# Where K and Q projections stand among the short convolutions of an encoder layer, and two small edits at the start and in the feed-forward part

## The chip, the core and the metric

The kernel runs on one core of a Trainium2 chip. Its engines work side by side, each on its own instruction stream: TensorE (matmuls, and transposes as matmuls), VectorE, ScalarE and GpSimd (element work), SyncE (which here issues the DMA transfers). The metric is the device time of one execution in microseconds (us). In the listings PE is TensorE, PEld its weight loads, DVE VectorE, ACT ScalarE, POOL GpSimd, and SPq SyncE's queue of transfers. L330 is line 330 of the kernel; lines of the changed kernel lie two or three higher, since the change adds lines.

## The reference

One encoder layer on 1024 tokens with 16 learned tokens set before them, width 1024, everything in 32-bit floats:

```python
h_res = concat([meta, x])                       # 1040 x 1024
h = rmsnorm(h_res, norm1_w)
proj = h @ w_in                                 # q k v z | beta, a | sc_b sc_c sc_x | gate_a gate_b
# branch A, per head (8 heads of 128), forward and backward:
qkv = silu(conv5(concat[q, k, v])); q, k = l2norm(q) * 128**-0.5, l2norm(k)
beta = sigmoid(b_raw); g = -exp(A_log) * softplus(a_raw + dt_bias)
o = scan(forward) + flip(scan(backward))        # chunks of tokens, state S 128 x 128:
    #   v_new = u - w @ S;  o_c = q_dec @ S + qk @ v_new;  S = S * gl + k_dec.T @ v_new
o_dn = rmsnorm(o) * dn_norm_w * silu(z)
# branch B and the merge
y_b = sc_b * conv3(sc_c * sc_x)
merged = sigmoid(gate_a) * (o_dn @ w_branch_dn) + sigmoid(gate_b) * (y_b @ w_branch_sc)
h_res += merged @ w_out
gu = rmsnorm(h_res, norm2_w) @ w_gate_up        # 2 x 2816 columns
h_res += (silu(gu[:, :2816]) * gu[:, 2816:]) @ w_down
out = rmsnorm(h_res, final_norm_w)[16:]
```

## The kernel before

**Precision.** A 32-bit product is done as three matmuls of a reduced type: each operand is split in a high part (a cast, on ScalarE) and a low part (the original less the high part, on VectorE; helper `split`, L86 and L87), and high x high, high x low and low x high are summed. So each piece of weights or activations passes both element engines once before TensorE can use it.

**Stages.** (1) The start: nine tiles of tokens are loaded, their root mean square taken (`root`, ScalarE and GpSimd), scaled in place (`scaled`, VectorE, L1019), transposed on TensorE (`turned`, L83) and split (`highs`, `lows`, L1038 and L1044). (2) The first part: all columns of the input projection, the convolutions, the scans of branch A. (3) One late gate (`dense`, L119 to L121) and the products of the branches and of the merge, in seven block products (`seven`, L1379). (4) The output projection and second norm (L1593 to L1595). (5) The feed-forward part, first half: 22 units of 128 pairs of hidden columns, each with seven products (`product`, L1653 to L1655). (6) Second half: the product with `w_down` (L1808 to L1810), also in seven block products, and the last norm.

**The first part** is emitted in an order that a planner in the kernel works out when the program is built: the manual schedule keeps it, and each engine runs its instructions in that order. The planner has a clock per engine (`T`), advanced by estimated costs. The projection is cut into *units* of 128 columns: for each of 8 heads a K, a Q and a V unit (`u_qkv`, numbers i = 0, 1, 2), and *fill units*: z per head, then for each of 8 column blocks three units of the short convolution (`u_short`, i = 0, 1, 2: the factor under the convolution, its partner, and the factor outside), then the gates (`u_gate`). `pick` (L921) chooses the next unit. In the kernel before it takes the next K, Q or V unit when `qkv_ok` allows it, and never between the three units of one short convolution (`mid`). `qkv_ok` lets a head begin only below `near + 3`, where `near` counts the scans that have reached round `NEAR`.

While a unit's matmuls are emitted (`dense_steps`, L330, eight steps per chunk of tokens), the planner sets pieces of other work between the steps: `run_streams` emits the streams of branch A (decay, norms, the triangular inverse, and the scan `g_scan` in 8 rounds per head), and `pump` (L296) emits VectorE work from four lanes: `conv` (the five-tap convolution of a K, Q or V unit, L353), `short` (the three-tap one), `fs` and `norm`. Among the lanes that are ready `pump` takes the one on which the least time has been spent so far. A third short-conv unit reads the finished convolution when its product is read out, and emits what is left of it at once if need be (`force`). The weights of a unit are fetched two units ahead, and split in four parts during the unit before (`split_part`, casts L941 on ScalarE and differences L938 on VectorE).

A round of the scan does, on TensorE, S times K and S times Q (L794, L797); on VectorE the rest `r` for both directions (L804); on TensorE the product with the inverse (L812); on ScalarE two scalings (L819 and the one after); on TensorE the two products L829 and L832; on VectorE the new state (L841) and the sums of the output. After the last round the output is scaled by its norm (L891, ScalarE), after a fixed delay of the planner's clock (L886), transposed (L83), multiplied with the gate z (L897) and stored (L900).

**Down sums.** In the feed-forward part, units 2 to 12 also prepare differences of rows of `w_down` for the last stage: `down_sums` (L1671) loads two rows of 128 x 1024 into a tile `sums`, does four differences on VectorE (L141) and stores them. Behind the first part the framework's scheduler sets each engine's order, by when it reckons an instruction's inputs ready: it may put work of a later unit ahead, and a new tile may be loaded as soon as its memory is free, so the first `down_sums`, which stand in the code of unit 2, are found among the instructions of unit 0. In units 0, 1 and 2 VectorE also makes the sums and differences of the unit's own weights (`sums`, L141 on `raw`; line L1631 for the first) and their splits.

## Time and profile before

| what | us |
|---|---|
| time, median of 3 runs | 1969.58 (1968.12 to 1970.8) |
| profiled execution | 1968.53 |
| its span, first to last instruction | 1966.8 |
| TensorE busy | 1943.5 (99%) |
| VectorE busy | 1468.4 (75%) |
| ScalarE busy | 868.7 (44%) |
| GpSimd busy | 159.2 (8%) |

The mean granted clock of TensorE is 0.999. The page gives the busy time of each engine; a table by windows gives it for stretches of the span; the waits are given by the instruction that waited, what released it, the total, how often and the longest; a timeline has, for each instruction or run of like instructions, the start, the duration, the engine, the line, what is written and read, and in brackets how long the engine stood idle before it and who released it. Matmuls are pipelined: a matmul of 512 columns is listed with some 0.39 us while the next one starts 0.23 us after it. So time lost between two matmuls is read from their starts: the distance, less what it is at full rate.

### The profile page before, as it was taken

How to read it: one execution, taken by the hardware profiler on the slowest of the kernel's cores; microseconds unless marked ns; L12 is line 12 of the kernel's file. 1: busy time of each engine (PE TensorE's matmuls, PEld its weight loads, DVE VectorE, ACT ScalarE, POOL GpSimd, SP SyncE). 2: the span in 40 equal slices, each digit the busy share in tenths (PEclk: the TensorE clock that was granted, in tenths of full speed). 3: DMA queues.
4: the chain of work that ended last, by engine and by line, in shares of the span. 5: the costliest groups of instructions: out<-in, count | busy, mean ns of one | idle time of the engine just before them, and what ended most of it. 6: DMA issues, size and time to landing. Idle time of an engine off the chain costs nothing.

```text
span 1966.8 us, 31940 instructions
## 1 busy us (share of the span) xinstructions
PE 1943.5 (99%) x11962; PEld 1703.1 (87%) x11962; DVE 1468.4 (75%) x2801; ACT 868.7 (44%) x2013; POOL 159.2 (8%) x457
## 2 busy tenths in 40 slices
PE   8999999999999999999999999999999999999998
PEld 8998899999999999998878888887888888888887
DVE  4778787879788878777458798559876887856574
ACT  5563554555555464533345545234332332324343
POOL 3012112011020202010000000000000000000001
PEclk9999999999999999999999999999999999999999
DMA  4222332323122223225287523333655545587654
GB/s 145 67 76 81 103 97 60 87 60 86 50 90 65 79 56 87 66 70 173 76 295 268 202 95 118 110 126 123 231 195 194 187 157 171 173 280 240 195 178 159
DMA packets 243136, 264.11 MB, mean 134 GB/s; under 512 B 46820, under 2 KB 166933, under 8 KB 240549
## 3 DMA queue, kind: packets, MB, share of 16 engines
q1 hardware_dynamic: 242981, 262.07, 41.8%
q8 instruction: 94, 1.54, 0.3%
q14 instruction: 61, 0.50, 0.1%
HBM read 189.58 MB, written 72.44 MB: 133 GB/s over the span
## 4 chain that ended last, share of the span: by engine, by line
PE 93%; DVE 3%; ACT 2%; issue 1%; DMA 0%; POOL 0%; SPq 0%; POOLq 0%; DVEq 0%; ACTq 0%
PE pm L330 34%; PE pm L1379 5%; PE pd L1379 4%; PE pe L1379 3%; PE pm L1653 2%; PE pm L1655 2%; PE pm L1654 2%; PE pd L1653 2%; PE pd L1655 2%; PE pd L1654 2%; PE pe L1655 2%; PE pe L1653 2%; PE pe L1654 2%; PE pd L812 2%; PE pe L581 2%; PE pm L1809 1%
## 5 line engine op out<-in xcount | busy, mean ns | idle before, releaser
L330 PE MATMUL pm<-hTh,wh 128*128 128x320 f32 (+4 forms) x1328 | 485.2, 366 | 0.1
L330 PE MATMUL pm<-hTh,wl 128*128 128x320 f32 (+4 forms) x1328 | 451.0, 340 | 0.0
L330 PE MATMUL pm<-al,wh 128*128 128x320 f32 (+4 forms) x1328 | 450.3, 340 | 0.5 <-DVE al L1044 0.5
L330 PEld LDWEIGHTS pm<-hTh,wl 128*128 128x128 f32 x1328 | 249.4, 188 | 15.4
L330 PEld LDWEIGHTS pm<-hTh,wh 128*128 128x128 f32 x1328 | 250.7, 189 | 13.5 <-ACT hTh L1038 0.2
L330 PEld LDWEIGHTS pm<-al,wh 128*128 128x128 f32 x1328 | 250.8, 189 | 13.1 <-DVE al L1044 0.7
L87 DVE TENSOR_TENSOR al<-raw,ring_h 128x1024 fp32r<-128x1024 f32 x73 | 88.4, 1223 | 64.3 <-ACT ring_h L86 54.6
L86 ACT CAST ring_h<-raw 128x1024 fp32r<-128x1024 f32 x73 | 76.8, 1053 | 110.4 <-PE pd L1810 35.7
L938 DVE TENSOR_TENSOR wl<-raw,wh 128x512 fp32r<-128x512 f32 x122 | 84.0, 690 | 45.7 <-ACT wh L941 45.1
L353 DVE SCALAR_TENSOR_TENSOR kq<-ra,wc,kq 128x520 f32<-128x520 f32 (+1 forms) x128 | 96.4, 753 | 3.0 <-ACT kq L387 1.2
L819 ACT ACTIVATE w<-pd,small 128x128 f32<-128x128 f32 x128 | 40.0, 364 | 97.1 <-PE pd L812 81.3
L128 POOL TENSOR_SCALAR ss<-ss 128x1 f32<-128x1 f32 x13 | 4.6, 351 | 934.8 <-ACT b L1820 605.0
L489 DVE TENSOR_TENSOR tm<-fP,fN 128x135 f32<-128x135 f32 (+23 forms) x248 | 72.2, 291 | 8.8 <-POOL mP L661 2.5
L493 DVE TENSOR_TENSOR fP<-fP,tm 128x135 f32<-128x135 f32 (+23 forms) x248 | 71.7, 289 | 7.4
L941 ACT CAST wh<-raw 128x512 fp32r<-128x512 f32 x122 | 74.5, 618 | 0.9 <-PE pm L330 0.8
L86 ACT CAST raw<-pair 128x1024 fp32r<-128x1024 f32 (+1 forms) x42 | 41.7, 993 | 56.5 <-PE pd L1379 26.0
L87 DVE TENSOR_TENSOR wl<-pair,wh 128x1024 fp32r<-128x1024 f32 (+1 forms) x42 | 48.2, 1148 | 22.3 <-ACT wh L86 22.2
L841 DVE SCALAR_TENSOR_TENSOR S<-S,eGl,pd 128x128 f32<-128x128 f32 x104 | 31.9, 345 | 43.9 <-PE pd L829 29.6
L87 DVE TENSOR_TENSOR raw<-pair,raw 128x1024 fp32r<-128x1024 f32 (+1 forms) x42 | 48.2, 1147 | 19.4 <-ACT raw L86 19.3
L130 POOL TENSOR_TENSOR small<-small,minus_half 128x9 f32<-128x9 f32 x16 | 29.9, 1870 | 404.8 <-DVE small L876 251.6
L86 ACT CAST wh<-pair 128x1024 fp32r<-128x1024 f32 (+1 forms) x42 | 41.7, 992 | 43.6 <-PE pd L1379 23.2
L1334 DVE TENSOR_TENSOR b<-pm,b 128x512 f32<-128x512 f32 x58 | 39.1, 686 | 21.2 <-PE pm L1655 19.0
(659 smaller groups left out, 4950.0 us busy)
## 6 DMA issues: line engine op xcount, KB each, us to landing
raw<-in_w_in_dram SPq DMA_DIRECT2D x64, 512.0 KB
raw<-in_w_gate_up_dram SPq DMA_DIRECT2D x44, 512.0 KB
sums<-in_w_down_dram SPq DMA_DIRECT2D x22, 512.0 KB
t_d<-sums SPq DMA_DIRECT2D x11, 1024.0 KB
raw<-s_d SPq DMA_DIRECT2D x44, 256.0 KB
raw<-t_d SPq DMA_DIRECT2D x44, 256.0 KB
act_d<-b SPq DMA_DIRECT2D x43, 256.0 KB
raw<-act_d SPq DMA_DIRECT2D x33, 256.0 KB
```

The lines of the kernel that those rows point to most:

```text
L86: nc.scalar.copy(hi, src)
L87: nc.vector.tensor_tensor(out=lo, in0=src, in1=hi.bitcast(F32), op=ALU.subtract)
L330: mm(po[:, :n], (wl if j == 2 else wh)[:, k], xl[k][:, t0:t0 + n] if j == 1 else xh[k][:, t0:t0 + n], start=(i == 0), stop=(i == 3 * KT - 1))
L353: nc.vector.scalar_tensor_tensor(out=acc, in0=raw[:, h0 + t:h0 + t + hn], scalar=wc[:, t, col:col + 1], in1=acc, op0=ALU.mult, op1=ALU.add)
L489: nc.vector.tensor_tensor(out=tv, in0=fP[:, 0:r, j:j + 1].broadcast_to([P, r, n]), in1=fN[:, j:j + 1, j + 1:32].broadcast_to([P, r, n]), o ...
L493: nc.vector.tensor_tensor(out=fP[:, 0:r, j + 1:32], in0=fP[:, 0:r, j + 1:32], in1=tv, op=ALU.subtract)
L938: nc.vector.tensor_tensor(out=u[1][1][:, k], in0=u[2][:, k], in1=u[1][0][:, k].bitcast(F32), op=ALU.subtract)
L941: nc.scalar.copy(u[1][0][:, k], u[2][:, k])
L1379: mm(bank[t], a[:, c], b, start=fresh, stop=first and k == 3 and j == 2, skip_group_check=not first)
L1653: mm(po, ah[:, k], bhk, start=k == 0, stop=False)
L1654: mm(po, ah[:, k], blk, start=False, stop=False)
L1655: mm(po, al[:, k], bhk, start=False, stop=k == 3)
```

## The change

It has four groups of edits.

1. *Order in the first part.* `pump` leaves the lane `short` aside whenever another lane is ready. K and Q units may now stand between the three units of a short convolution, a V unit still not. `near` counts scans that reached round 3 instead of 5, so that a head's units may begin earlier. A K unit takes its two tiles after its first chunk's matmuls instead of before them.
2. *Output of a head.* The delay before the last scaling on the planner's clock is 2300 instead of 1500.
3. *Start.* The first three tiles of tokens are scaled in two halves of 512 columns.
4. *Down sums.* The first `down_sums` (of unit 2) writes two elements of its new tile from `sg`, the result of that unit, before it loads the tile; so this load, and all that follows it in that tile, comes after that result.

```diff
@@ pump
+            if len(cand) > 1 and "short" in cand:
+                cand.remove("short")
             k = min(cand, key=lambda q: spent[q])
@@ u_qkv
-        if i == 0:
-            while freed < h - 2:
-                T["pe"] += 100
-                yield
-            st_["kq"] = d1.tile([P, 2, L], F32, tag="kq", name=uid("kq"), bufs=3)
-            st_["vT"] = d1.tile([P, L], F32, tag="vT", name=uid("vT"), bufs=2)
...
             yield from dense_steps(po, w, hx, t0, n, sweep=(h == i == ci == 0))
             if raw is None:
+                if i == 0:
+                    while freed < h - 2:
+                        T["pe"] += 100
+                        yield
+                    st_["kq"] = d1.tile([P, 2, L], F32, tag="kq", name=uid("kq"), bufs=3)
+                    st_["vT"] = d1.tile([P, L], F32, tag="vT", name=uid("vT"), bufs=2)
+                dst = (st_["kq"][:, 0], st_["kq"][:, 1], st_["vT"])[i]
@@ g_scan
-        yield T["dve"] + 1500
+        yield T["dve"] + 2300
@@ units
-    NEAR = 5
+    NEAR = 3
@@ pick
-        if qkv_units and not mid and qkv_ok():
+        if qkv_units and qkv_ok() and not (mid and qkv_units[0][3] == 2):
@@ scaled
-            nc.vector.scalar_tensor_tensor(out=xs[t][:p], in0=xs[t][:p], scalar=rss[t][:p, 1:2], in1=w1row[:p],
-                                           op0=ALU.mult, op1=ALU.mult)
+            for c in (slice(0, 512), slice(512, 1024)) if t < 3 else (slice(0, D),):
+                nc.vector.scalar_tensor_tensor(out=xs[t][:p, c], in0=xs[t][:p, c], scalar=rss[t][:p, 1:2], in1=w1row[:p, c],
+                                               op0=ALU.mult, op1=ALU.mult)
@@ down_sums
-    def down_sums(k):
+    def down_sums(k, behind=None):
...
+        if behind is not None:
+            nc.scalar.copy(r[:1, :, 0:1], behind[:1, 0:2].unsqueeze(2))
@@ loop over the feed-forward units
-            down_sums(j - 2)
+            down_sums(j - 2, sg if j == 2 else None)
```

With these, the order of units per head goes from S0 S1 S2 K Q V to S0 S1 K Q S2 V in the middle of the first part (S0 to S2 are the three units of a short convolution). Three places are shown as each engine has its instructions in order.

The first is VectorE in the V unit of a head in the middle of the first part, at one round of the scan: L804 makes r, L938 is the low half of the next unit's weights, L489 and L493 are steps of the norm stream, L865 a sum of the output. Before:

```order
L865 TENSOR_TENSOR NP_1845<-pd_4201,NP_1845 128x128
L489 TENSOR_TENSOR tm_4287<-fP_3804,fN_3803 128x136
L938 TENSOR_TENSOR wl_4168<-raw_3925,wh_4167 128x512
L804 SCALAR_TENSOR_TENSOR r_657_4299<-pd_4293,negEG,vS_3437 128x128
L804 SCALAR_TENSOR_TENSOR r_658_4301<-pd_4293,negEG,vS_3437 128x128
L493 TENSOR_TENSOR fP_3804<-fP_3804,tm_4287 128x8x17
```

And in the changed kernel, at the V unit of the same head:

```order
L867 TENSOR_TENSOR NP_1848<-pd_4084,NP_1848 128x128 x2
L491 TENSOR_TENSOR tm_4163<-fP_3865,fN_3864 128x184
L806 SCALAR_TENSOR_TENSOR r_619_4177<-pd_4168,negEG,vS_3463 128x128
L806 SCALAR_TENSOR_TENSOR r_620_4179<-pd_4168,negEG,vS_3463 128x128
L495 TENSOR_TENSOR fP_3865<-fP_3865,tm_4163 128x8x23
L940 TENSOR_TENSOR wl_4106<-raw_3939,wh_4105 128x512
```

The weight difference stood ahead of both r; now it stands behind them.

The second is SyncE at the end of the first part: L455 stores a gate, L900 the last head's output, L810 loads z, L1343 loads the first blocks of the branch products. Before:

```order
L455 DMA tb_d_99<-rb_12191 128x512
L810 DMA vS_11402<-z_d_108 128x1024
L455 DMA tb_d_99<-rb_12250 128x512
L900 DMA o_d_116<-NP_10419 128x4x128 x2
L1343 DMA pair_12285<-in_w_in_dram 128x4x512
```

And in the changed kernel:

```order
L457 DMA tb_d_98<-rb_12175 128x512
L902 DMA o_d_116<-NP_10325 128x4x128 x2
L457 DMA tb_d_98<-rb_12222 128x512
L457 DMA tb_d_99<-rb_12250 128x512
L457 DMA tb_d_99<-rb_12278 128x512
L1346 DMA pair_12288<-in_w_in_dram 128x4x512
```

The output's two stores stood last before the block's load; now three gate stores lie between them. On TensorE 3 projection matmuls followed the last L832 of the last scan; now 99 do, and the last head's eight transposes, which stood among the late gate's matmuls, stand among these.

The third is VectorE at the passage from unit 0 to unit 1 of the feed-forward part: L1334 adds a product's bank to a running sum, L1657 multiplies the sum by its SiLU gate, L1631 and L141 on `raw` are the sums of unit 1's weights, and L87 on `s_hl` is the low half of these. Before:

```order
L1334 TENSOR_TENSOR b_2391_14775<-pd_14932,b_2391_14775 128x512
L1631 TENSOR_TENSOR raw_14815<-raw_14815 128x512
L1657 TENSOR_TENSOR b_2391_14775<-b_2391_14775 128x512
L1334 TENSOR_TENSOR b_2391_14775<-pd_14933,b_2391_14775 128x512 x2
L141 TENSOR_TENSOR raw_14815<-raw_14814,raw_14815 128x512
L87 TENSOR_TENSOR w_2418_14911<-raw_14852,w_2418_14911 128x512
L1334 TENSOR_TENSOR b_2391_14775<-pd_14934,b_2391_14775 128x512
L141 TENSOR_TENSOR raw_14814<-raw_14815,raw_14814 128x512
L87 TENSOR_TENSOR s_hl_15006<-raw_14815,s_hl_15006 128x1024
```

And in the changed kernel:

```order
L1634 TENSOR_TENSOR raw_14818<-raw_14818 128x512
L141 TENSOR_TENSOR raw_14818<-raw_14817,raw_14818 128x512
L1337 TENSOR_TENSOR b_2391_14778<-pd_14935,b_2391_14778 128x512
L141 TENSOR_TENSOR raw_14817<-raw_14818,raw_14817 128x512
L1660 TENSOR_TENSOR b_2391_14778<-b_2391_14778 128x512
L1337 TENSOR_TENSOR b_2391_14778<-pd_14936,b_2391_14778 128x512 x2
L141 TENSOR_TENSOR raw_14817<-raw_14817 128x512
L1337 TENSOR_TENSOR b_2391_14778<-pd_14937,b_2391_14778 128x512
L87 TENSOR_TENSOR s_hl_15009<-raw_14818,s_hl_15009 128x1024
```

The sums of the weights on `raw` stand one or two additions earlier, and two steps of down sums (L141 on `sums`) that stood just ahead of the piece shown are gone from there.

More of the change, by code (lines that the diff above doesn't have):

```diff
@@ L367, in u_qkv @@
         st_ = heads[h]
-        if i == 0:
-            while freed < h - 2:
-                T["pe"] += 100
-                yield
-            st_["kq"] = d1.tile([P, 2, L], F32, tag="kq", name=uid("kq"), bufs=3)
-            st_["vT"] = d1.tile([P, L], F32, tag="vT", name=uid("vT"), bufs=2)
         col = (8 + h, h, 16 + h)[i]
-        dst = (st_["kq"][:, 0], st_["kq"][:, 1], st_["vT"])[i]
         raw = None
```

## The prediction, on record before the changed kernel ran

> **What bounds the kernel now.** I read the first part of the page, then the busy time of each engine by stage, then the waits of TensorE in total, and last the order of time at each wait. The profiled execution took 1968.53 us; its span is 1966.8 us, and 1.7 us lie around it.
>
> ```profile
> span 1966.8 us, 31940 instructions
> PE 1943.5 (99%) x11962; PEld 1703.1 (87%) x11962; DVE 1468.4 (75%) x2801; ACT 868.7 (44%) x2013; POOL 159.2 (8%) x457
> ```
>
> TensorE is the bound. The change adds and removes no matmul, so it can only win back time in which TensorE stood still. Where that time lies, by stage (start, first part with the projections, three branch products, entry of the feed-forward part, rest):
>
> ```profile
> 0.00:16.00 16.00, 11.14 (x81) 10.19 (x81) 6.69 (x10) 9.40 (x16) 5.35 (x15) 1.00 0.91 282
> 16.00:1002.00 986.00, 977.63 (x7613) 902.05 (x7613) 750.35 (x1897) 492.44 (x1536) 138.31 (x410) 1.00 0.29 82
> 1002.00:1340.00 338.00, 337.83 (x1525) 280.53 (x1526) 258.08 (x296) 155.29 (x204) 7.44 (x16) 1.00 0.50 170
> 1340.00:1362.00 22.00, 19.07 (x80) 14.31 (x80) 22.00 (x32) 8.18 (x13) 0.00 (x0) 1.00 0.19 62
> 1362.00:1967.00 605.00, 597.82 (x2667) 495.99 (x2665) 431.29 (x570) 203.43 (x249) 8.13 (x17) 1.00 0.60 199
> ```
>
> The columns are TensorE, its weight loads, VectorE, ScalarE and GpSimd busy, then the clock. TensorE's idle time is 4.9, 8.4, 0.2, 2.9 and 7.2 us; the clock is full everywhere. The last 7.2 us are the end of the program, which no edit touches. What is left to win is about 16 us, under 1%. In the fourth row VectorE is busy for all 22 us: there it is the bound. The waits by whom TensorE waited for (total, times, longest):
>
> ```profile
> PE pd L812 <- DVE r L804: 2.9, 5, 1.0
> PE pd L83 <- DVE xr L1019: 2.6, 3, 1.4
> PE pe L1653 <- ACT mA L86: 1.0, 1, 1.0
> ```
>
> **The change, part by part.** *First part: pump's rule, the place of K and Q units, NEAR.* These move instructions; none is added. A round of the scan needs VectorE's r before its product L812:
>
> ```profile
> 350.38 0.31 PE L330 MATMUL pm<-al,wh 128*128 128x320 f32 x1
> 350.53 0.31 PE L330 MATMUL pm<-hTh,wl 128*128 128x320 f32 x1
> 350.55 0.69 DVE L938 TENSOR_TENSOR wl<-raw,wh 128x512 fp32r<-128x512 f32 x1 [1.60 <-ACT wh L941]
> 351.16 0.60 DVE L804 SCALAR_TENSOR_TENSOR r<-pd,negEG,vS 128x128 f32<-128x128 f32 x2
> 351.81 0.60 PE L812 MATMUL pd<-r,NP 128*128 128x128 f32 x3 [0.98 <-DVE r L804]
> 452.88 0.60 PE L812 MATMUL pd<-r,NP 128*128 128x128 f32 x3 [0.98 <-DVE r L804]
> ```
>
> VectorE stood idle for 1.60 us behind a weight split L938 whose ScalarE half came late (ScalarE first emptied a chunk of V), and r stood behind it. The lost time is more than 0.98: starts at full rate are 350.53 - 350.38 = 0.15 us apart, here 1.28, so 1.13 was lost. The Trainium skill (Perfetto Trace Analysis, Identifying the Most-Contended Engine) says that matmul busy time misleads because matmuls are pipelined; the trace agrees, by 0.15 us a wait, and with the idle column alone the sum below would be some 1.2 us smaller.
>
> Two of the five waits on r are of this make (2 x 1.13 = 2.3); the other three come to 2.9 - 1.96 + 3 x 0.15 = 1.4. In the changed order r goes ahead of that split in the V unit of head 3, and in no round does the split's cast stand behind both row copies. So the 2.3 go; I keep the 1.4 and grant 0.3 for new ones: **-2.0**. Bounds: all five vanish (-3.7), or, with 40 rounds of heads 3 to 7 newly placed, as much again appears (+3.7). I take a value near the first, for the make of the largest waits is gone.
>
> The short convolutions now run last, and up to six steps of one are forced at once before its third unit's product is read out. Six steps at the mean of the nearest row (0.75 us) are 4.5 us, in which the second half of that unit gives TensorE 24 x 0.227 = 5.4 us of work: nothing. Without that cover one burst would cost up to 4.5, and three are this long. The tiles' allocation behind K's first chunk issues nothing. Weight loads of the moved units keep their distance of two units on SP's queue: nothing.
>
> ```profile
> L353 DVE SCALAR_TENSOR_TENSOR kq<-ra,wc,kq 128x520 f32<-128x520 f32 (+1 forms) x128 | 96.4, 753 | 3.0 <-ACT kq L387 1.2
> ```
>
> *The seam to the branch products.* The last head's output, the late gate and the first block of the next stage meet here:
>
> ```profile
> 987.62 0.58 ACT L453 ACTIVATE rb<-pm 128x512 f32<-128x512 f32 x1
> 988.50 0.39 PE L119 MATMUL pm<-hTh,wh 128*128 128x512 f32 x1
> 990.36 0.62 PE L83 MATMUL pd<-ident,NP 128*128 128x128 f32 x2 [1.48 <-ACT NP L891]
> 992.49 1.54 SPq L900 DMA_DIRECT2D o_d<-NP  x2
> 996.13 2.22 SPq L1343 DMA_DIRECT2D pair<-in_w_in_dram  x4
> 999.76 0.39 PE L120 MATMUL pm<-al,wh 128*128 128x512 f32 x1
> 999.98 0.39 PE L121 MATMUL pm<-hTh,wl 128*128 128x512 f32 x1
> 1002.17 0.47 PE L1379 MATMUL pm<-hTh,raw 128*128 128x512 f32 x1 [1.80 <-issue]
> ```
>
> Two holes: 990.36 - 988.50 - 0.23 = 1.63, waiting for the head's scaling, and 1002.17 - 999.98 - 0.23 = 1.96, waiting for the block's load, which could start only when the output stores had landed (2.1 us after their issue ended at 994.03) and freed the memory. In the change 99 projection matmuls follow the last scan round where 3 did, and the output goes out before the last three gate stores. The first hole's 1.63 goes. The load now hangs on the last gate store. From the last projection matmul's start: 0.39 to its end, 0.58 eviction, 0.32 issue, 2.1 to land, then 1002.17 - 996.13 = 6.04 to the first product: 9.4 us. TensorE has that matmul and 48 of the late gate, 49 x 0.227 = 11.1. Margin 1.7: the second hole goes too. **-3.6**; bound on the other side -1.6.
>
> *Halves of the first tiles.*
>
> ```profile
> 6.56 0.23 POOL L128 TENSOR_SCALAR rs<-rs 128x1 f32<-128x1 f32 x1 [5.15 <-ACT jk_first L1014]
> 10.43 1.28 DVE L1019 SCALAR_TENSOR_TENSOR xr<-xr,rs,w1row 128x1024 f32<-128x1024 f32 x1 [1.67 <-POOL rs L130]
> 10.81 0.98 POOL L128 TENSOR_SCALAR rs<-rs 128x1 f32<-128x1 f32 x1 [0.42 <-ACT jk_first L1014]
> 12.48 1.28 DVE L1019 SCALAR_TENSOR_TENSOR xr<-xr,rs,w1row 128x1024 f32<-128x1024 f32 x1 [0.17 <-POOL rs L130]
> 13.42 1.06 ACT L1097 CAST wh<-raw 128x1024 fp32r<-128x1024 f32 x1
> 14.51 1.07 ACT L1038 CAST hTh<-pd 128x512 fp32r<-128x512 f32 x2
> 15.93 1.51 PE L330 MATMUL pm<-hTh,wh 128*128 128x336 f32 x8
> ```
>
> Two halves cost 2 x 0.75 - 1.28 = 0.2 us more on VectorE, but the first transposes can start 0.5 earlier. TensorE's 2.6 us of waiting is not the price: before 15.93 nothing but these tiles can run, and ScalarE is the chain (weight cast at 13.42, tile 2's casts right behind). Tile 1's casts move up by about 0.45, the weight cast with them, and tile 2's casts follow: **-0.4**. Bounds: -0.8 (tile 2's half-tile lead counts too), +0.2 (the second half sets the pace).
>
> GpSimd's L128 took 0.98 instead of 0.23 while VectorE's L1019 ran, and ended as that did. By the Trainium skill (SBUF — State Buffer, Terms, shared port pair) the loser fully blocks for the whole instruction; the trace agrees. With a seam in the middle GpSimd may take the port between the halves and hold the second back by its 0.23; by that rule this term is -0.2.
>
> *The down sums tied to the third unit's result.*
>
> ```profile
> 1353.42 0.69 DVE L141 TENSOR_TENSOR sums<-sums 128x512 f32<-128x512 f32 x1
> 1357.04 0.68 DVE L141 TENSOR_TENSOR raw<-raw,raw 128x512 f32<-128x512 f32 x1
> 1357.68 0.39 PE L1655 MATMUL pd<-b,mB 128*128 128x512 f32 x1
> 1357.76 1.05 ACT L86 CAST s_hl<-raw 128x1024 fp32r<-128x1024 f32 x1 [3.33 <-DVE raw L141]
> 1358.24 0.69 DVE L1334 TENSOR_TENSOR b<-pd,b 128x512 f32<-128x512 f32 x1
> 1358.85 0.50 PE L1653 MATMUL pe<-s,s_hl 128*128 128x512 f32 x1 [0.78 <-ACT s_hl L86]
> 1359.44 1.22 DVE L87 TENSOR_TENSOR s_hl<-raw,s_hl 128x1024 fp32r<-128x1024 f32 x1
> 1360.71 0.50 PE L1655 MATMUL pe<-s,s_hl 128*128 128x512 f32 x1 [1.12 <-DVE s_hl L87]
> ```
>
> Lost here: 1358.85 - 1357.68 - 0.23 = 0.94, and 1360.71 less its predecessor's start and 0.23, which is 1.12 + 0.16 = 1.28: together 2.2. In the change no sums stand before the split of s_hl, and the first raw L141 moves from after the additions to before them, so the first cast is early and its 0.94 goes. Late next is the second half's cast: its last L141 still stands behind two additions, so it ends near 1358.9, some 0.5 after TensorE wants it. VectorE's first s_hl cannot start before the addition that reads a product ending at 1358.07, so it is done near 1359.9: about 0.2 more. **-1.5**; bounds -2.2 and 0. The wait on mA (1.0) lies ahead of all this and stays. On SP the tied load stands directly behind the store of the same result, so it blocks nothing new; the sums' consumers come after 22 units and the last sums are stored about half way. The new copy of two elements on ScalarE is covered, as that engine is busy for 203 of the last 605 us.
>
> **Sum.** -2.0 - 3.6 - 0.4 - 1.5 = **-7.5 us** of 1968.53, which gives 1961.0. That execution lies 1.05 us under the median of the runs shown, 1969.58; against it, 1962.1. I forecast **1962**.
>
> **Rivals.** *A, the waits on r come back elsewhere:* the heads stand closer together, so VectorE has less slack per round. For it: the same work ends earlier. Against: VectorE is busy for 750 of 986 us there. First part at 0 instead of -2.0: 1964.1; at +3.7: 1967.8. *B, the block's load is still late at the seam:* the margin of 1.7 us goes if the last gate store or the load itself takes longer, the other loads crowding it. Then the second hole stays: 1964.0. *C, slower:* one mechanism, r late in many rounds of heads 3 to 7, because convolution steps now go ahead of all else but the norm and stand in front of r. A late round costs 2.9/5 + 0.15 = 0.73 us. To lose 0.2% after gains of 5.5 it takes 9.4/0.73 = 13 more late rounds of the 40; with 16 the time is 1969.6 - 5.5 + 11.7 = 1976. Today 5 of 64 rounds are late. *D, the tie or the halves change nothing* and A holds as well: 1969.6 - 3.6 = 1966.
>
> **How the numbers follow.** About 0.2%, 4 us, is what a measurement of this kernel can tell from no change, so faster means under 1965.6 and slower over 1973.5. Forecast 0.50 (faster), A 0.21 (0.12 faster, 0.09 same), B 0.12 (0.09 faster, 0.03 same), C 0.09 (0.07 slower, 0.02 same), D 0.08 (0.03 faster, 0.05 same). Faster 0.74, same 0.19, slower 0.07. The likeliest case has 1959.3 (all terms at their best, -10.3) to 1965. The range 1958.5 to 1968 takes in A, B and D and leaves out C.
>
> **What will show it.** Right: no hole over 0.5 us between the last projections and the first L1379, and the transposes of the last head inside the gate's matmuls; waits of L812 on r under 2 us in total; no sums of VectorE between 1345 and 1362, one wait of about 0.5 there; first projection matmul at 15.5. Wrong: a wait on r in more than ten rounds, or a wait of L1379 on the load.

## The result and the profile after

The changed kernel takes 1961.14 us, median of 5 runs (1960.82 to 1961.57), against 1969.58 (1968.12 to 1970.8) before: a ratio of 0.9958, with a 95% interval of 0.9947 to 0.9968. It is faster by 0.42%, and 0.9 us below the forecast of 1962. The profiled execution took 1961.08 us, with a span of 1959.4.

The first part of the page, and the busy time by stage, for windows that answer to those shown of before (moved by 6 us behind the first part):

```profile
span 1959.4 us, 31938 instructions
PE 1941.7 (99%) x11962; PEld 1704.4 (87%) x11962; DVE 1468.1 (75%) x2804; ACT 867.9 (44%) x2014; POOL 158.4 (8%) x457
...
0.00:16.00 16.00, 11.91 (x81) 10.17 (x81) 6.95 (x13) 9.86 (x16) 5.45 (x15) 1.00 0.94 283
16.00:996.00 980.00, 975.10 (x7613) 903.78 (x7613) 750.24 (x1900) 491.47 (x1536) 137.32 (x410) 1.00 0.29 83
996.00:1334.00 338.00, 338.00 (x1528) 280.29 (x1527) 256.59 (x293) 154.73 (x202) 7.48 (x16) 1.00 0.49 168
1334.00:1356.00 22.00, 20.31 (x87) 15.57 (x86) 21.81 (x30) 9.15 (x13) 0.00 (x0) 1.00 0.06 19
```

The busy times of all engines are as before, to 2 us. The stretch of the first part is 6 us shorter at the same 7613 matmuls, and its idle time fell from 8.4 to 4.9 us. The other 2.5 us stand in the column of busy time (977.63 before, 975.10 now): the listing hides a part of each wait behind a matmul (0.98 us listed for 1.13 lost, in the prediction's working), so waits are read from starts below. The entry of the feed-forward part has 1.7 us of idle time where it had 2.9. The waits of TensorE (waiting instruction, releaser: total, times, longest):

```profile
PE pd L714 <- ACT T L708: 1.7, 1, 1.7
...
PE pe L83 <- DVE al L1047: 1.0, 1, 1.0
...
PE pm L1656 <- ACT s_hl L86: 0.7, 1, 0.7
PE pd L814 <- DVE r L806: 0.5, 2, 0.3
```

The waits on r (L812 before, L814 now) fell from 2.9 to 0.5. The waits on the output's scaling and on the first block's load are gone. One new wait stands at the top, 1.7 us of L714 on ScalarE.

By the starts of TensorE's instructions: the first projection matmul starts at 15.96 (15.93 before), the first branch product at 996.31 (1002.17), the first feed-forward product at 1318.44 (1324.32), the first product with w_down at 1741.96 (1749.38), the last at 1948.54 (1955.98). So the stages went from 986.24 to 980.35, from 322.15 to 322.13, from 425.06 to 423.52 and from 206.60 to 206.58: -5.9 in the first part and its seam, -1.5 in the first half of the feed-forward part, nothing elsewhere. The sum is -7.4, as is the difference of the spans.

The seam now:

```profile
985.20 0.39 PE L332 MATMUL pm<-hTh,wl 128*128 128x512 f32 x1
985.68 0.60 ACT L455 ACTIVATE rb<-pm 128x512 f32<-128x512 f32 x1 [4.84 <-PE pm L332]
986.30 0.32 SPq L457 DMA_DIRECT2D tb_d<-rb  x1
988.48 2.29 SPq L1346 DMA_DIRECT2D pair<-in_w_in_dram  x4
996.08 0.39 PE L121 MATMUL pm<-hTh,wl 128*128 128x512 f32 x1
996.31 0.39 PE L1382 MATMUL pm<-hTh,raw 128*128 128x512 f32 x1
```

The last gate's store is issued 1.1 us behind the last projection matmul and the load 2.2 us behind that store; the branch product follows the late gate's last matmul after 0.23 us, without a hole. Between 985.20 and 996.31 stand 11.1 us of matmuls.

And the split of unit 1's weights:

```profile
1352.17 1.05 ACT L86 CAST s_hl<-raw 128x1024 fp32r<-128x1024 f32 x1 [2.55 <-DVE raw L141]
1352.23 0.39 PE L1657 MATMUL pe<-s,s_hl 128*128 128x512 f32 x1
1353.27 0.50 PE L1656 MATMUL pm<-mA,s_hl 128*128 128x512 f32 x1 [0.65 <-ACT s_hl L86]
```

One hole is left there, 1353.27 - 1352.23 - 0.23 = 0.81, where there were 0.94 and 1.28.

The start, where nothing was won:

```profile
9.67 1.06 ACT L1016 ACTIVATE jk_first<-xr 128x1024 f32<-128x1024 f32 x1 [0.21 <-DMA xr<-in_x_dram]
10.90 0.39 POOL L128 TENSOR_SCALAR rs<-rs 128x1 f32<-128x1 f32 x1 [0.48 <-ACT jk_first L1016]
12.39 1.40 DVE L1022 SCALAR_TENSOR_TENSOR xr<-xr,rs,w1row 128x512 f32<-128x512 f32 x2
14.05 1.14 ACT L1041 CAST hTh<-pd 128x512 fp32r<-128x512 f32 x2
14.98 0.74 DVE L1047 TENSOR_TENSOR al<-pe,hTh 128x256 fp32r<-128x256 f32 x2
15.82 0.21 PE L83 MATMUL pe<-ident,rows 25*128 25x25 f32 x1 [0.97 <-DVE al L1047]
15.96 0.42 PE L332 MATMUL pm<-hTh,wh 128*128 128x336 f32 x1
```

ScalarE's last casts ahead of the first matmul begin 0.46 us earlier than before (14.05 against 14.51), just as forecast. But the matmul stands behind a small transpose (L83 on `rows`, which turns the convolution weights), and that waits for a bank that VectorE frees with L1047 at 14.98 + 0.74 = 15.72. Before, the same places were:

```profile
14.94 0.75 DVE L1044 TENSOR_TENSOR al<-pe,hTh 128x256 fp32r<-128x256 f32 x2
15.79 0.21 PE L83 MATMUL pe<-ident,rows 25*128 25x25 f32 x1 [0.78 <-ACT hTh L1038]
```

The view of before names ScalarE's cast as the releaser, which ended at 15.58; but VectorE's instruction on the same bank ended later, at 15.69, and the transpose started 0.10 behind it, as it does in the changed kernel. Before, the two engines were thus done 0.11 us apart, and moving ScalarE alone could win little.

### The profile page after: what moved, and what is told of

Its sections match the earlier page's. It is cut to its first block, busy times and chain, and to the rows that moved or that the text cites. A ratio compares the mean times of both kernels' runs of the same rounds, so it can differ in the third digit from the quotient of the medians.

```text
span 1959.4 us, 31938 instructions
## 1 busy us (share of the span) xinstructions
PE 1941.7 (99%) x11962; PEld 1704.4 (87%) x11962; DVE 1468.1 (75%) x2804; ACT 867.9 (44%) x2014; POOL 158.4 (8%) x457
## 3 DMA queue, kind: packets, MB, share of 16 engines
q8 instruction: 94, 1.54, 0.3%
## 4 chain that ended last, share of the span: by engine, by line
PE 89%; DVE 5%; ACT 3%; issue 1%; DMA 1%; POOL 0%; SPq 0%; POOLq 0%; DVEq 0%; ACTq 0%
PE pm L332 31%; PE pm L1382 5%; PE pd L1382 4%; PE pe L1382 3%; PE pm L1656 3%; PE pm L1658 3%; PE pm L1657 2%; PE pd L1658 2%; PE pd L1656 2%; PE pd L1657 2%; PE pe L1658 2%; PE pe L1656 2%; PE pe L1657 2%; PE pm L1814 1%; PE pm L1815 1%; PE pm L1813 1%
## 5 line engine op out<-in xcount | busy, mean ns | idle before, releaser
L332 PE MATMUL pm<-hTh,wh 128*128 128x512 f32 (+4 forms) x1328 | 483.8, 365 | 0.1
L332 PE MATMUL pm<-hTh,wl 128*128 128x512 f32 (+4 forms) x1328 | 450.5, 340 | 0.0
L332 PE MATMUL pm<-al,wh 128*128 128x512 f32 (+4 forms) x1328 | 449.6, 339 | 0.5 <-DVE al L1047 0.5
L87 DVE TENSOR_TENSOR al<-raw,ring_h 128x1024 fp32r<-128x1024 f32 x73 | 88.4, 1223 | 63.6 <-ACT ring_h L86 63.2
L128 POOL TENSOR_SCALAR ss<-ss 128x1 f32<-128x1 f32 x13 | 4.6, 353 | 951.1 <-ACT b L1825 603.4
L87 DVE TENSOR_TENSOR raw<-pair,raw 128x1024 fp32r<-128x1024 f32 (+1 forms) x42 | 48.0, 1143 | 30.4 <-ACT raw L86 30.4
L87 DVE TENSOR_TENSOR wl<-pair,wh 128x1024 fp32r<-128x1024 f32 (+1 forms) x42 | 48.1, 1144 | 21.7 <-ACT wh L86 21.6
L661 POOL TENSOR_TENSOR tm<-mP,mN 1x15 f32<-1x15 f32 (+7 forms) x120 | 37.3, 311 | 237.0 <-DMA mN<-ndm 228.7
```

What stands on the lines that cost most here:

```text
L87: nc.vector.tensor_tensor(out=lo, in0=src, in1=hi.bitcast(F32), op=ALU.subtract)
L332: mm(po[:, :n], (wl if j == 2 else wh)[:, k], xl[k][:, t0:t0 + n] if j == 1 else xh[k][:, t0:t0 + n], start=(i == 0), stop=(i == 3 * KT - 1))
```

## The experiments

Lost time below is the distance of two starts less that distance at full rate (0.227 us behind a matmul of 512 columns, and the median of the kernel before for each other kind). The *first stretch* is the time from the first projection matmul's start to the first branch product's.

### Each part alone

The order edits and the longer delay alone (the changed kernel, with these two lines taken back):

```diff
-            for c in (slice(0, 512), slice(512, 1024)) if t < 3 else (slice(0, D),):
+            for c in (slice(0, D),):
...
-            down_sums(j - 2, sg if j == 2 else None)
+            down_sums(j - 2)
```

> The changed kernel with the tiles scaled whole and the down sums untied, so the order edits and the longer delay alone. If the four groups of edits act apart, as the two traces say (first projection matmul to first branch product 986.2 us before, 980.4 in the changed kernel; 424.06 + 1 to 423.5 in the feed-forward first half), it takes 1969.6 - 5.9 = 1963.7 us, keeps 980.4 for that stretch and shows the 0.94 and 1.3 us of lost time at the split of s_hl again. Rival: part of the 5.9 hangs on the start or on the tie; then it stays above 1964.5.

It took 1964.33 us (ratio 0.9976, 0.9968 to 0.9985); the first stretch is 980.66, and the holes at the split of s_hl are 0.97 and 1.30. So the 5.6 of that stretch belong to these edits, and more than that: this profile has a price in it that the changed kernel's profile has not. Behind the hole at L714, which is 1.84 us in both and has 1.2 us of matmuls of 32 x 32 behind it, the granted clock falls here (the third column from the end):

```profile
494.00:497.00 3.00, 3.00 (x10) 3.00 (x11) 2.83 (x6) 2.91 (x12) 0.00 (x0) 0.52 0.66 179
```

Ten matmuls of 384 columns start 0.32 us apart there instead of 0.17, some 1.5 us. The time is 0.6 above the expected 1963.7; that the clock is the reason is likely, and the section on the clock below says what is known of it.

The halves alone (that one edit, in the kernel before):

> The kernel before with the first three tiles scaled in halves and nothing else. Theory from the changed kernel's trace: VectorE sets the start, since the last bank that the transposes of the convolution weights need is freed by its subtraction L1044, and halves cost it 0.13 us a tile; so the first projection matmul starts 6.2 to 6.4 us after the third tile's square begins, as before (9.57 to 15.93), and the time is 1969.6, within 0.3. Rival, the prediction's step: ScalarE is the chain and the 0.4 was hidden by a first tile that landed 0.25 us later in that one profile; then the distance is 5.9 to 6.0 and the time 0.3 to 0.4 lower.

1969.61 us (ratio 1.0001, 0.9992 to 1.001). The first projection matmul starts 6.34 us after the third tile's square (9.57 to 15.91), against 6.36 before. The halves win nothing, and not because a tile came late.

The tie alone, in the kernel before (the two elements are written ahead of the two loads, as in the change), and then the tie behind the loads, where the loads stay at their old place and the order on VectorE changes as with the tie. The second, whose edit is shown, overwrites two elements of the loaded rows, so it is for timing alone:

```diff
         nc.sync.dma_start(r[:, 0], w_down[k * P:k * P + P, :])
         nc.sync.dma_start(r[:, 1], w_down[(HK + k) * P:(HK + k + 1) * P, :])
+        if behind is not None:
+            nc.scalar.copy(r[:1, :, 0:1], behind[:1, 0:2].unsqueeze(2))
```

> The kernel before with the first down sums tied to the third unit's result and nothing else. Theory: 1969.6 - 1.5 = 1968.1, one wait of 0.7 to 0.8 us at the split of s_hl in place of 0.94 and 1.3 us lost. Rival: the 1.5 came with the other edits (the stage starts 6 us earlier in the changed kernel); then 1969.6.

> As the one before, but the two elements are written after the loads of the tile, so that the two loads stay where they were and only the four differences on VectorE come late; VectorE's order is that of the tied kernel, instruction by instruction. It leaves two elements of the rows of w_down wrong. If VectorE's time ahead of the split of s_hl was the price, it gains the same 1.5: 1968.1 and a single wait of 0.7 to 0.8. If the loads' traffic or their place in SyncE's queue was the price, it gains nothing: 1969.6 and waits of 0.8 and 1.1 as before.

1967.20 us (ratio 0.9989, 0.998 to 0.9997) and 1967.39 (0.9993, 0.9984 to 1.0001); the first half of the feed-forward part takes 423.52 and 423.53 us in their profiles, as in the changed kernel (423.52), with one hole of 0.80 and 0.81. The two medians lie 2.0 and 1.9 us under that of the kernel before beside them (1969.24); the interval of the second just reaches 1, so its reading rests on the stage in its profile. There, with the loads at their old place, the same is won, so the price was the two differences of down sums on VectorE, and neither the traffic nor SyncE's queue.

### A price behind the holes: the clock

The profiles of the order edits alone and of the halves alone show 426.63 and 426.60 us for that stage where the kernel before had 425.06, with the same holes. Windows of 3 us (TensorE, its weight loads, VectorE, ScalarE, GpSimd busy, then the granted clock), of the halves-only kernel and of the kernel before:

```profile
1357.00:1360.00 3.00, 1.83 (x7) 0.86 (x5) 3.00 (x6) 1.68 (x2) 0.00 (x0) 1.00 0.17 66
1360.00:1363.00 3.00, 2.25 (x5) 1.82 (x6) 3.00 (x5) 1.04 (x1) 0.00 (x0) 0.63 0.25 67
1363.00:1366.00 3.00, 3.00 (x12) 2.43 (x11) 3.00 (x5) 1.05 (x1) 0.00 (x0) 0.80 0.74 231
```

```profile
1357.00:1360.00 3.00, 1.81 (x7) 0.86 (x5) 3.00 (x6) 1.68 (x2) 0.00 (x0) 1.00 0.16 61
1360.00:1363.00 3.00, 2.29 (x10) 1.80 (x10) 3.00 (x6) 1.05 (x1) 0.00 (x0) 1.00 0.28 68
1363.00:1366.00 3.00, 3.00 (x15) 2.50 (x14) 3.00 (x6) 1.06 (x1) 0.00 (x0) 1.00 0.72 224
```

The holes are equal, but in the first the clock falls behind them, and some eight matmuls start 0.43 us apart instead of 0.23: 8 x 0.2 = 1.6 us on top of the 2.2. It happens in some executions of one program and not in others. Of the 33 runs of the kernel before beside this group, 17 have a mean granted clock of 0.998 or less and 16 one of 0.999; the 16 runs at 0.998 take 1969.82 in the mean, the 16 at 0.999 1968.22: 1.6 us again. 8 of 11 runs of the order edits alone, which have the place at L714 as well, and 5 of 11 of the halves alone are at 0.998; of the 22 runs of the two ties, none. The two holes of this stage are not the only ones that do it: the kernel with the old place of K and Q, below, has the tie, and its profile shows the clock at 0.55 from 811 to 814 us, behind a hole of 2.9 us at L583; 4 of its 11 runs are at 0.998. Nor is the clock the only source of scatter: the 16 runs at 0.999 lie between 1967.16 and 1969.98, the 22 of the ties between 1966.00 and 1969.01. The Trainium skill (TensorE: Matmul & The Clock Gate, What's actually happening) says that the gate watches a free-running window of about 3.4 us, so that its moment shifts from run to run, and grants half rate when idle; the halved rate and the changing runs agree, and so does the length: the first table has (0.37 + 0.20) x 3 = 1.7 us of clock missing, which is 3.4 us at half rate. A table of the same page of the Trainium skill (Why this matters for your kernels) asks for no idle gap over some 3 us. Here two gaps of 0.94 and 1.3 us, 0.5 us of work apart, were enough in some runs, and in two profiles so was one of 1.84, with 1.2 us of small matmuls (32 x 32) behind it. Where the clock fell in runs without a profile is inferred from their mean clock, not seen.

### Each order edit taken back

In the changed kernel, one edit at a time; the four pieces below are four kernels: the old place of K and Q units, NEAR at 5, the old choice of VectorE's lanes, and the old delay:

```diff
-        if qkv_units and qkv_ok() and not (mid and qkv_units[0][3] == 2):
+        if qkv_units and not mid and qkv_ok():
...
-    NEAR = 3
+    NEAR = 5
...
-            if len(cand) > 1 and "short" in cand:
-                cand.remove("short")
...
-        yield T["dve"] + 2300
+        yield T["dve"] + 1500
```

> The changed kernel with the old rule of the place of K and Q units (never between the units of a short convolution). By its order 9 projection matmuls follow the last scan round where the change has 99 and the kernel before 3; 15 matmuls lie between that round and the first transpose of the last output (14 before). If those 90 matmuls closed the seam, its two holes come back, some 1.4 us each (1.63 and 1.96 before), and r stands right behind a split whose cast is behind both row copies in 5 rounds (6 before, 2 in the change), so the lost time at L812 rises from 1.4 to some 3: in all 1961.1 + 2.8 + 1.6 = 1965.5 us. Rival: the longer delay or NEAR closed the seam; then it stays at 1961 to 1963.

> The changed kernel with NEAR at 5 again. By its order 51 projection matmuls follow the last round, 23 of them before the first transpose (5.2 us; the scaled output is ready some 5.9 us after that round), and a gate's store follows the output's, so the block's load hangs on the gate as in the change. Theory: a first hole of 0 to 0.7 us, no second; L812 loses some 2.5 (4 rounds of the bad make): 1961.1 + 0.4 + 1.1 = 1962.6. Rival: the heads' closer spacing carries the first part's gain; then the seam is as before, 1964.7 or more.

> The changed kernel with the old choice of VectorE's lanes (short convolutions not put last). By its order 39 projection matmuls follow the last round, 27 of them before the first transpose (6.1 us), and the output's stores are again the last before the block's load: from the last transpose, some 1.0 us behind the last projection matmul, 9.6 us to the first product (992.58 to 1002.17 before), 10.6 in all against the gate's 11.1 and the transposes. Theory: no hole of over 0.5 at the seam, L812 loses some 2.0 (3 rounds of the bad make): 1961.1 + 0.6 = 1961.7. Rival: the lane rule is what feeds TensorE, since the convolutions of K, Q and V come sooner; then 1964 or more.

> The changed kernel with the delay of the head's output at 1500 again. At the seam only three matmuls' place changes, so it stays closed. If the delay matters it is within heads 0 to 6: an output's transposes that stand too early make TensorE wait for L893, as in the 1.63 of the kernel before. Theory: no such wait over 0.3, 1961.1 within 0.7. Rival: the transposes of the earlier heads wait, some 0.5 us each for seven heads: 1964.5.

| kernel | time, us | ratio to before (95%) | first stretch | lost at the seam | lost at L812/L814 |
|---|---|---|---|---|---|
| before | 1969.1 | 1 | 986.24 | 3.6 | 4.2 |
| changed | 1961.14 | 0.9958 (0.9947 to 0.9968) | 980.35 | 0 | 1.4 |
| old place of K, Q | 1966.58 | 0.9988 (0.9979 to 0.9996) | 985.91 | 2.1 | 3.3 |
| NEAR 5 | 1959.00 | 0.9949 (0.9935 to 0.9962) | 978.22 | 0 | 2.1 |
| old lane rule | 1961.80 | 0.9963 (0.995 to 0.9975) | 980.67 | 0 | 1.1 |
| delay 1500 | 1963.78 | 0.9973 (0.9962 to 0.9983) | 983.58 | 0 | 2.1 |

(The changed kernel's time is from another group of runs, with 1969.58 before. The later taking of a K unit's two tiles was not taken back by itself.) How much of such a difference one profile can carry is shown by four kernels whose first part has the same order on VectorE and ScalarE, the halves themselves aside: the kernel before, the halves alone and the two ties have first stretches of 986.24, 986.16, 985.03 and 986.29, which is 1.3 us of scatter.

*The place of K and Q units* carries nearly the whole gain: without it both holes of the seam are back (1.39 and 0.67, expected 1.4 each), as are the two large waits on r (1.27 and 1.14). Its profile also has the fall of the clock at 811 us, at most 1.7 us of its 985.91; by the medians it is 5.4 us above the changed kernel. The other waits of that kernel, and of the one with the shorter delay:

```profile
PE pe L583 <- DVE PQ L617: 2.8, 1, 2.8
PE pd L814 <- DVE r L806: 2.5, 3, 1.1
...
PE pd L83 <- ACT NP L893: 1.2, 1, 1.2
```

```profile
PE pe L583 <- DVE PQ L617: 1.5, 1, 1.5
...
PE pd L714 <- issue: 1.2, 2, 0.7
...
PE pd L796 <- DVE S L843: 0.9, 1, 0.9
...
PE pe L83 <- ACT jk L545: 0.7, 1, 0.7
```

*The delay* is worth some 3 us, but neither as expected nor as the rival had it: no transpose waits for its scaling; instead five other places, the inverse L714, the state L796 and the norms' products L583 among them, lose 0.65 to 1.6 each. Not all of it is the delay's: L796 (at 235 us) loses 0.73 in the changed kernel's profile too; and it loses nothing with NEAR at 5, but 1.1 in a kernel that differs from that one only in its start and in the feed-forward part. That a shift of a few instructions sets new coincidences is the likely reading; their sum could not be read from the edit. *The lane rule* is worth 0.3 in the stretch, within the scatter of such coincidences. *NEAR at 3* seems to cost up to 2: with 5, the 1.84 lost at L714 (491 us) is not there, a wait on r of 1.27 is back, and the 51 matmuls behind the last round close the seam as well as 99. NEAR 5 is the fastest version run; its interval overlaps that of the changed kernel, and the two were not timed side by side, so the 2.1 us rest on the two traces and the two ratios. Two later kernels with NEAR at 5 (*The start without its bank*, below) took 1961.0, as the changed kernel does, so what NEAR is worth stays open between 0 and 2 us.

### The seam's chain, uncovered

The late gate made a unit of the first part:

```diff
-LATE = 9
+LATE = 8
```

> The changed kernel with the late gate made a unit of the first part (one gate fewer behind it), so that nothing covers the load of the first block of the branch products; the work is the same. The chain of the prediction from the last projection matmul's start: 0.39 + 0.58 eviction + 0.32 issue + 2.1 landing + 6.04 from the load's issue to the first product = 9.4 us, a hole of 9.2 at that place, and as TensorE idles far longer than the 2.2 us after which the granted clock stood at 0.51 for 3 us in the first-part-only kernel, 1.6 us more behind it: 1961.1 + 9.2 + 1.6 = 1972. Rival: the load doesn't hang on the last gate's store, and its 6.04 was the queue behind it; then a hole of 4 to 6 us, 1966 to 1968.

```profile
997.25 0.39 PE L332 MATMUL pm<-hTh,wl 128*128 128x512 f32 x1
997.72 0.60 ACT L455 ACTIVATE rb<-pm 128x512 f32<-128x512 f32 x1 [4.84 <-PE pm L332]
998.34 0.32 SPq L457 DMA_DIRECT2D tb_d<-rb  x1
1000.69 2.13 SPq L1346 DMA_DIRECT2D pair<-in_w_in_dram  x4
1006.06 0.62 ACT L86 CAST raw<-pair 128x512 fp32r<-128x512 f32 x1 [7.75 <-DMA pair<-in_w_in_dram]
1006.78 0.76 PE L1382 MATMUL pm<-hTh,raw 128*128 128x512 f32 x1 [9.15 <-ACT raw L86]
```

1973.21 us (ratio 1.002, 1.001 to 1.003). From 997.25 to 1006.78 are 9.53 us, a hole of 9.30 where 9.2 were expected, and the matmuls behind it start 0.43 us apart until 1010.3: the clock, as expected. (The time is 1.2 above the expected 1972. Its profile has two more losses: the clock falls behind the hole at L714 once more, 0.67 and 0.76 in the windows of 494 to 497 and 497 to 500 us, and there is a hole of 1.58 us at 1112, whose cause was not traced.) So the load does hang on the last gate's store, and from the load's issue to the first product it takes 6.09 us. In the changed kernel that makes 988.48 + 6.09 = 994.57, which is 1.74 us before the product is wanted.

### The slower rival's mechanism, made large

The lane of the short convolutions never chosen, so that all of each is forced at once:

```diff
-            cand = [k for k, q in lanes.items() if q and q[0].ready <= now + 20 + DEP * (k == "fs")]
+            cand = [k for k, q in lanes.items() if k != "short" and q and q[0].ready <= now + 20 + DEP * (k == "fs")]
...
-            if not cand and any(q and q[0].ready <= now + DEP + 20 for q in lanes.values()):
+            if not cand and any(q and q[0].ready <= now + DEP + 20 for k, q in lanes.items() if k != "short"):
...
-            if len(cand) > 1 and "short" in cand:
-                cand.remove("short")
```

> The changed kernel with the lane of the short convolutions never chosen, so that all six steps of each are forced at once when the first half of its third unit is read out: eight bursts of six (in the change 3, 5, 6 and 1 steps, four without any). The prediction: 4.5 us of VectorE are covered by the second half's 5.4 us of matmuls, so no burst costs over 0.3; the order leaves 9 projection matmuls behind the last scan round, as in the run with the old place of K and Q, so the seam loses its 2.1 again: 1961.1 + 2.1 = 1963 to 1965. The slower rival: r and the other short steps of the scans stand behind the bursts, 2 to 4 us each, eight times: 1975 or more, with waits of TensorE on VectorE at the eight places.

1966.86 us (ratio 0.9987, 0.9978 to 0.9996). A burst of six in the trace of VectorE:

```profile
527.39 0.47 DVE L404 TENSOR_SCALAR rb<-ra,cols 128x512 f32<-128x512 f32 x1
527.90 1.54 DVE L409 SCALAR_TENSOR_TENSOR rb<-ra,cols,rb 128x512 f32<-128x512 f32 x2
529.36 0.48 DVE L404 TENSOR_SCALAR rb<-ra,cols 128x512 f32<-128x512 f32 x1
529.88 1.54 DVE L409 SCALAR_TENSOR_TENSOR rb<-ra,cols,rb 128x512 f32<-128x512 f32 x2
531.33 0.68 DVE L444 TENSOR_TENSOR rb<-pm,rb 128x512 f32<-128x512 f32 x1
```

It takes 3.94 us. From its start to 3 us behind its end, TensorE loses nothing over 0.1 us in six of the eight bursts, and 0.9 and 0.6 us in the other two: 1.5 in all, against the rival's 2 to 4 each. The seam loses 2.0 by its order (1.39 and 0.58). The time stands 1.9 above the upper expected value; the largest hole of the stretch outside the seam is 1.59 us at a transpose (L83, 488 us), near no burst, and the kernel with the old lane rule has one of 1.57 at the same line; the rest (985.43 in all) was not taken apart. In the changed kernel none of the bursts of three and more costs anything over 0.1 us.

### The start without its bank

The changed kernel with NEAR at 5, the two transposes of the convolution weights behind the first 24 matmuls, and the first operand of unit 1 split in two halves; and the same with the tiles scaled whole:

```diff
-    NEAR = 3
+    NEAR = 5
...
-        pt = psd()
-        transpose(pt[:, :120], rows[:120, 0], 120)
-        pt2 = psd()
-        transpose(pt2[:, :25], rows[:25, 1], 25)
         root(3)
         steps(gen0)
+        pt = psd()
+        transpose(pt[:, :120], rows[:120, 0], 120)
+        pt2 = psd()
+        transpose(pt2[:, :25], rows[:25, 1], 25)
...
-            split(sh, sl, r)
+            for q in ((slice(0, 4), slice(4, 8)) if j == 1 and i == 0 else (slice(0, 8),)):
+                split(sh[:, q], sl[:, q], r[:, q])
```

> The changed kernel with NEAR at 5, the two transposes of the convolution weights moved behind the first unit's first 24 matmuls, and the split of the first operand of unit 1 in two halves. Theory: the start no longer waits for the bank that VectorE frees; the first projection matmul starts 5.6 to 5.8 us after the third tile's square begins instead of 6.3, -0.5; at the split of s_hl 0.2 to 0.8 less is lost; near5 had 1959.0, so 1958.0. Rival: VectorE, which is busy without a gap from 12.4 us on, holds the next matmuls (low halves) back by what the first ones gain; then the start gains nothing.

> As the one before with the first three tiles scaled whole. If the halves lead the transposes and ScalarE's casts by some 0.4 us and only the bank hid it, this is 0.3 to 0.4 us slower than the one before and its first projection matmul starts 0.3 to 0.4 later after the third tile's square. If VectorE's extra 0.13 a tile weighs as much, there is no difference.

```profile
9.61 1.06 ACT L1016 ACTIVATE jk_first<-xr 128x1024 f32<-128x1024 f32 x1 [0.19 <-DMA xr<-in_x_dram]
14.66 1.51 PE L332 MATMUL pm<-hTh,wh 128*128 128x336 f32 x8
20.47 0.37 PE L1053 MATMUL pe<-hTh,wba 128*64 128x336 f32 x1 [1.09 <-DVE wba L1119]
```

```profile
9.64 1.06 ACT L1016 ACTIVATE jk_first<-xr 128x1024 f32<-128x1024 f32 x1 [0.19 <-DMA xr<-in_x_dram]
15.19 1.04 PE L332 MATMUL pm<-hTh,wh 128*128 128x336 f32 x5 [0.24 <-ACT hTh L1041]
```

With the bank out of the way the first matmul starts 5.05 us after the third tile's square with halves and 5.55 without, where it was 6.3: the halves do lead by 0.5, and the bank hid it; here the first matmul waits for ScalarE's cast, as the prediction had it. But the start gains nothing from it: the copies of the turned weights and the cast of `wba` now come later on ScalarE, and the small gates (L1053) wait 1.09 for them. The 25th projection matmul starts 14.15 and 14.21 us after the third tile's square, where it is 13.41 with NEAR 5 alone. The times are 1961.04 (ratio 0.9956, 0.9944 to 0.9969) and 1960.94 (0.9957, 0.9944 to 0.9969), two us above NEAR 5 alone, with first stretches of 981.07 and 979.34 against 978.22 (they begin earlier; the first branch product comes at 995.74 and 994.52, against 994.39). So the start accounts for some 0.8 of the two us; the rest is not explained. Of the other edit, the finer split, 0.25 us arrive (423.26 and 423.23 us for the stage, 423.48 in NEAR 5). So this was no improvement.

## Why the prediction was right, step by step

**The bound** held: TensorE is still busy for 99% of the span with the same matmuls, and what was won is, by the starts, time in which it stood still.

**First part, -2.0:** measured -5.9 with the seam; less the seam's 3.6, it is -2.3. The step was right in its make: the two waits of 1.14 behind a late weight split are gone, and r loses 1.4 where it lost 4.2. It is right in its sum partly by luck: 0.3 was granted for new waits, and one alone, L714 at 491 us, lost 1.84, while other places (L712 and L780 before) lost their 0.7 each, and profiles of one order differ by 1.3 in this stretch, so that -2.0 and -2.3 agree says little. The waits on r were put at 3.7 in all, from the five listed; by the starts there are seven, with 4.2. And the sentence that no split's cast stands behind both row copies was not exact: the order has two such rounds left (444 and 542 us), which cost nothing.

**The bursts, nothing:** right, and shown: none in the changed kernel costs over 0.1 us, and eight full ones cost 1.5 together. Six steps take 3.94 us, not 4.5, as two of them are plain scalings of 0.47.

**The seam, -3.6:** right in mechanism and size. Both holes are gone. The chain was put at 9.4 us and measures 9.5 without cover; the margin was put at 1.7 and is 1.7.

**The halves, -0.4:** wrong. The step that failed is "ScalarE is the chain". ScalarE's casts did move up by 0.46; but the first matmul stands on TensorE behind a transpose whose bank is freed by VectorE's L1047, and VectorE, with no gap from 12.39 us on, has 0.13 us more to do per halved tile (1.41 against 1.28). The halves alone, where the time did not move, and the start without its bank, where the halves lead by 0.5, show it. The lower end of the bounds (the second half sets the pace, +0.2) had the right engine for another reason. The rule of the Trainium skill on the shared port (SBUF — State Buffer, Terms) is borne out on GpSimd's side: L128, 0.98 before, took 0.39 (10.90) and ended at 11.29, 0.08 behind the first half, as it had ended 0.08 behind the whole tile. That VectorE's second half is held back for it is not seen: the pair takes 1.41 with GpSimd there (10.46) and without (7.72).

**The down sums, -1.5:** right: -1.54, by VectorE's time alone, with the one wait left where it was expected ("the second half's cast", 0.81 lost against 0.5 + 0.2). What the step missed is the clock behind the holes. It is the likely reason why the medians differ by 8.4 while the two profiled executions differ by 7.4: the kernel before loses another 1.6 us in about half of its runs, which is 0.8 in the mean, and in the five runs of the changed one the mean clock is 0.999.

**The rivals.** A came partly true (new waits on r of 0.29 and 0.35 us, and L714) and was outweighed. B didn't occur, by 1.7 us. C's mechanism, made large, costs 0.2 us a burst in the mean and 0.9 at most; and taking the lane rule back leaves the waits on r about where they are (1.1 against 1.4 us). D holds for the halves and fails for the tie.

The forecast of 1962 thus has two errors of opposite sign: 0.4 us too much for the start, and 0.3 in the first part and about 1 too little that is put down to the clock. The closeness of the total owes something to that.

## What to carry to other kernels

Where one engine is busy 99% of the time, read what is lost from the distances of starts, list the few holes, and ask for each what is queued behind it: work that is known to be there at a seam (matmuls after the last dependent step, counted from the order) closes a hole at a price that can be worked out. An engine's earlier finish is worth nothing until the next instruction's every condition is looked at, its bank too. And take back each part of a change alone: here taking back one line of the order lost 5.4 us of the gain, while another (NEAR) may have cost up to 2 us.

## What the runs showed that was not expected

Short holes can cost more than their length: two of 0.94 and 1.3 us in a stretch of 3 us halved the granted clock for some 3 us in some runs of a program (0.51 and 0.63 in windows of 3 us) and left it at 1.00 in others, at 1.6 us each time. One hole of 1.84 us, at L714, with small matmuls behind it, did the same in the profiles of the order edits alone (0.52) and of the late gate as a unit (0.67 and 0.76 in two windows), and not in that of the changed kernel (1.00), which has the same hole: it too may lose 1.5 us there in some run, though its five stand at 0.999. The kernel before scatters by 4.4 us (1967.16 to 1971.57 in 33 runs), the changed kernel by 0.75 (1960.82 to 1961.57 in 5 runs); with so few runs, and with 3.0 us in the 22 of the ties, the clock is not shown to be the whole reason.
